# Softmax over rows of 512: sixteen equal chunks in two rings of buffers, replaced by seven unequal chunks worked in place in one array

## The chip, the cores and the metric

The kernel runs on one core of one Trainium2 chip. The metric is device microseconds for one execution of the kernel, taken as the median of several runs. A profile is a single execution; it has a span, from its first to its last instruction, and a time of its own, which is a little longer than the span.

## The reference

The input is 16 x 1024 rows of 512 float32 numbers, 33.55 MB. Each row is turned into its softmax, and an output of the same size is written.

```python
def reference(x: np.ndarray) -> np.ndarray:
    x_max = np.max(x, axis=-1, keepdims=True)
    exp_x = np.exp(x - x_max)
    return (exp_x / np.sum(exp_x, axis=-1, keepdims=True)).astype(np.float32)
```

## The kernel before, in words

The 16,384 rows are laid over 128 partitions, so each partition works on 128 rows. One "row" below means one row on every partition: 128 x 2 KB, 256 KB in HBM. The loop `for t in range(nchunks)` takes 16 chunks of R = 8 rows, 2 MB each. A chunk is contiguous in HBM, and a partition's share of it is one run of 16 KB.

For each chunk the loop records these steps, and the tile framework turns them into five instruction streams with semaphores between them:

- L47: SyncE (queue q1 of the profile) issues the load into `x_tile`, from a ring of 7 buffers.
- L49: GpSimd copies one column of the chunk into a guard tile. It waits for the load, and a later load of the same buffer waits for it.
- L61: ScalarE runs eight `activation` instructions, one for each row. Each computes exp of 512 numbers into `e_tile` (a ring of 4 buffers) and adds up the row in `accum_out`; the profile lists the reading of that sum as an instruction of its own. The bias is the constant 0.0: the maximum isn't subtracted, since `use_max` is off.
- L71, L74: VectorE takes the reciprocal of the eight sums, and multiplies all 4096 numbers of a partition by the broadcast reciprocals in one `tensor_mul`.
- L76: ScalarE's queue (q10) issues the store of `e_tile`.

After the loop, L80 has GpSimd write one column of the last four `e_tile` buffers, which waits for their stores. The framework's scheduler chooses the order on each engine: the built program has pairs of chunks on ScalarE, that is sixteen L61 instructions and then two stores. A load waits for the engines that read its buffer before, and a chunk's L61 waits until the store four chunks earlier has left its `e_tile`.

Of the kernel before, what the change touches and what calls it, by code (L numbers as in the profile page):

```python
# [2 lines left out]

# [4 lines left out]


@with_exitstack  # L10
def kernel(
    ctx: ExitStack,
    tc: tile.TileContext,
    x: bass.AP,
    out: bass.AP,
):
    nc = tc.nc
    P = nc.NUM_PARTITIONS

    x_flat = x.flatten_outer_dims()  # L20
    out_flat = out.flatten_outer_dims()
    n, d = x_flat.shape

    R = int(os.environ.get("SM_R", "8"))
    XBUFS = int(os.environ.get("SM_XBUFS", "7"))
    EBUFS = int(os.environ.get("SM_EBUFS", "4"))

    rows_per_chunk = P * R
    assert n % rows_per_chunk == 0
    nchunks = n // rows_per_chunk  # L30

    x_t = x_flat.rearrange("(t p r) d -> t p r d", p=P, r=R)
    out_t = out_flat.rearrange("(t p r) d -> t p r d", p=P, r=R)

    x_pool = ctx.enter_context(tc.tile_pool(name="xp", bufs=XBUFS))
    e_pool = ctx.enter_context(tc.tile_pool(name="ep", bufs=EBUFS))
    stats_pool = ctx.enter_context(tc.tile_pool(name="stats", bufs=12))
    guard_pool = ctx.enter_context(tc.tile_pool(name="guard", bufs=1))

    use_max = os.environ.get("SM_USEMAX", "0") == "1"  # L40

    guard_tile = guard_pool.tile([P, 1], mybir.dt.float32)

    e_tiles = []
    for t in range(nchunks):
        x_tile = x_pool.tile([P, R, d], mybir.dt.float32)
        nc.sync.dma_start(out=x_tile, in_=x_t[t])  # L47

        nc.gpsimd.tensor_copy(out=guard_tile, in_=x_tile[:, 0, 0:1])  # L49

        if use_max:
            neg_max = stats_pool.tile([P, R], mybir.dt.float32)
            nc.vector.reduce_max(
                out=neg_max, in_=x_tile, axis=mybir.AxisListType.X, negate=True
            )

        e_tile = e_pool.tile([P, R, d], mybir.dt.float32)
        e_tiles.append(e_tile)
        sums = stats_pool.tile([P, R], mybir.dt.float32)
        for r in range(R):  # L60
            nc.scalar.activation(  # L61
                out=e_tile[:, r, :],
                in_=x_tile[:, r, :],
                func=mybir.ActivationFunctionType.Exp,
                bias=neg_max[:, r : r + 1] if use_max else 0.0,
                scale=1.0,
                accum_out=sums[:, r : r + 1],
            )

        recip = stats_pool.tile([P, R], mybir.dt.float32)  # L70
        nc.vector.reciprocal(out=recip, in_=sums)  # L71

        recip_b = recip.unsqueeze(2).to_broadcast([P, R, d])
        nc.vector.tensor_mul(out=e_tile, in0=e_tile, in1=recip_b)  # L74

        nc.scalar.dma_start(out=out_t[t], in_=e_tile)  # L76

    for b in range(min(EBUFS, nchunks)):
        e_tile = e_tiles[nchunks - 1 - b]
        nc.gpsimd.memset(e_tile[:, 0, 0:1], 0.0)  # L80


# [1 line left out]
_INS = ['x']  # L84
_OUTS = [((16, 1024, 512), 'float32')]


# [23 lines left out]
```

## Time and profile before

| | before |
|---|---|
| median of 9 runs | 163.66 us (163.28 to 164.05) |
| the profiled execution's own time | 163.66 us |
| its span | 161.7 us |
| HBM read and written | 33.55 MB and 33.55 MB |
| VectorE busy | 74.0 us in 32 instructions |
| ScalarE busy | 80.7 us in 257 instructions |
| GpSimd busy | 13.7 us in 24 instructions |

How to read it: busy time is a sum over the span, and says little of what ends last. The page's second part cuts the span into 40 slices of 4.04 us; a digit is the busy share of a slice in tenths, "DMA" is the mean share of the core's 16 DMA engines, and "GB/s" is what these moved. The third part gives the share of each queue. The chain of the fourth part follows the last instruction back through what released it.

### The profile page before, as it was taken

Reading aid. Unit: us, or ns where it says so; the run is one execution under the profiler, and the core shown is the slowest. Engines: PE = TensorE matmul, PEld = TensorE weight load, DVE = VectorE, ACT = ScalarE, POOL = GpSimd, SP = SyncE. Lnnn points to the kernel's source line nnn. Section 1 sums busy time; section 2 is a strip of 40 time slices with the busy share of each in tenths; the row PEclk is TensorE's granted clock in tenths of the full one; section 3 lists DMA queues with packets and bytes.
Section 4 is the critical chain, followed back from the end, with each engine's and each line's share of the span. In section 5 each row is a group of like instructions: output and inputs, shape, how many; then the busy total and the mean of one; then the engine's idle time right before and its main releaser. Section 6 shows DMA issues by size and latency. Waiting matters only on the chain.

```text
span 161.7 us, 456 instructions
## 1 busy us (share of the span) xinstructions
DVE 74.0 (46%) x32; ACT 80.7 (50%) x257; POOL 13.7 (8%) x24
## 2 busy tenths in 40 slices
DVE  0006970994195509073000007950993399059700
ACT  3089519924883390910000099439915980896000
POOL 0000000024080000000000006300000000000000
DMA  5999999999999999999999999999999999999993
GB/s 154 430 434 418 442 341 440 434 426 434 430 422 442 430 426 438 422 434 442 422 434 442 422 430 442 422 434 432 430 434 426 430 438 426 430 434 426 434 438 154
DMA packets 4610, 67.13 MB, mean 415 GB/s; under 512 B 512, under 2 KB 512, under 8 KB 512
## 3 DMA queue, kind: packets, MB, share of 16 engines
q1 hardware_dynamic: 2304, 33.56, 49.4%
q10 hardware_dynamic: 2304, 33.56, 48.5%
q14 instruction: 2, 0.02, 0.0%
HBM read 33.55 MB, written 33.55 MB: 415 GB/s over the span
## 4 chain that ended last, share of the span: by engine, by line
DMA 52%; ACT 28%; DVE 17%; issue 1%; ACTq 1%; POOLq 0%; SPq 0%
DMA x_tile<-in_x_dram 35%; ACT e_tile L61 28%; DMA out_dram<-e_tile 17%; DVE e_tile L74 16%; DVE recip L71 1%; ACTq L76 1%; POOLq L106 0%; POOLq L80 0%; SPq L47 0%
## 5 line engine op out<-in xcount | busy, mean ns | idle before, releaser
L61 ACT ACTIVATE e_tile<-x_tile 128x512 f32<-128x512 f32 x128 | 78.5, 614 | 66.4 <-DMA x_tile<-in_x_dram 35.4
L74 DVE TENSOR_TENSOR e_tile<-e_tile,recip 128x4096 f32<-128x4096 f32 x16 | 70.8, 4425 | 0.6
L71 DVE RECIPROCAL recip<-sums 128x8 f32<-128x8 f32 x16 | 3.2, 203 | 78.0 <-ACT e_tile L61 78.0
L61 ACT ACTIVATION_READ_ACCUMULATOR e_tile<-x_tile 128x1 f32 x128 | 23.9, 187 | 0.0
L49 POOL COPY guard_tile<-x_tile 128x1 f32<-128x1 f32 x16 | 13.1, 819 | 124.1 <-DMA x_tile<-in_x_dram 124.1
L80 POOL MEMSET e_tile<- 128x1 f32 x4 | 0.4, 98 | 22.9 <-DMA out_dram<-e_tile 22.9
L61 ACT ACT_TABLE_LOAD x1 | 1.3, 1283 | 0.7 <-PEq L95 0.7
L95 POOL MEMSET const-float32-0.0<- 128x1 f32 x1 | 0.1, 98 | 0.2 <-issue 0.2
L95 POOL MEMSET const-bfloat16-1.0<- 128x1 bf16 x1 | 0.1, 101 | 0.0
L95 POOL MEMSET const-uint8-127<- 128x1 uint8 x1 | 0.1, 101 | 0.0
L95 POOL MEMSET const-float32-1.0<- 128x1 f32 x1 | 0.1, 98 | 0.0
## 6 DMA issues: line engine op xcount, KB each, us to landing
x_tile<-in_x_dram SPq DMA_DIRECT2D x16, 2048.0 KB, 42.3
out_dram<-e_tile ACTq DMA_DIRECT2D x16, 2048.0 KB, 17.9
```

The costliest lines, as they stand in the source:

```text
L49: nc.gpsimd.tensor_copy(out=guard_tile, in_=x_tile[:, 0, 0:1])
L61: nc.scalar.activation(out=e_tile[:, r, :], in_=x_tile[:, r, :], func=mybir.ActivationFunctionType.Exp, bias=neg_max[:, r : r + 1] if use_ ...
L71: nc.vector.reciprocal(out=recip, in_=sums)
L74: nc.vector.tensor_mul(out=e_tile, in0=e_tile, in1=recip_b)
L76: nc.scalar.dma_start(out=out_t[t], in_=e_tile)
L80: nc.gpsimd.memset(e_tile[:, 0, 0:1], 0.0)
L95: nc = _bacc.Bacc("TRN2", target_bir_lowering=False, num_devices=1)
```

## The change

The row maximum is computed and subtracted. The seven chunks have 3, 5, 9, 17, 31, 31 and 32 rows (`CHUNKS`: rows, and place in the array). One array `held` of 96 rows, 192 KB on each partition, holds the first six chunks side by side; the seventh lies over the first four (rows 0 to 31). A load is one DMA for a whole chunk, so a partition's run is 6 to 64 KB. Six loads are issued at the start (`EARLY`); the seventh is recorded behind the store of chunk 3 (`AFTER_STORE`).

Work is cut into groups of about eight rows: one each for chunks 0, 1 and 2, two for chunk 3 (8 and 9 rows), four for each of the last three (7, 8, 8, 8; the last 8, 8, 8, 8), 17 in all. `rowmax` is one VectorE reduction for a group, negated; `exps` is one `activation` for each row with that maximum as a bias read from memory, in place; `scale` is a reciprocal, and then one `tensor_scalar_mul` for each row, in place. The store of a chunk is issued from ScalarE's queue when its last group is scaled. The order is written out under `manual_schedule`: rowmax g, exps g, scale g-1. The GpSimd copies and memsets are gone.

In the built program VectorE has rowmax g, then the reciprocal and products of g-1, then rowmax g+1; ScalarE has the exponentials of g, then the store whose chunk ended with g-1. The seventh load waits on SyncE for the stores of chunks 0 to 3. The sixth waits there for the first load, whose semaphore it takes over. Waits go by the overlap of rows in `held`: rowmax waits for the load of its own chunk alone.

```diff
+CHUNKS = [(3, 0), (5, 3), (9, 8), (17, 17), (31, 34), (31, 65), (32, 0)]
+SBUF_ROWS = 96
+EARLY = 6
+AFTER_STORE = {3: [6]}
+GROUP = 8
...
+    held = data.tile([P, SBUF_ROWS, d], F32, name="held")
+    place = [held[:, s : s + R, :] for R, s in CHUNKS]
...
+        m = max(1, round(R / GROUP))
+        cuts = [R * i // m for i in range(m + 1)]
+        groups += [(k, a, b, b == R) for a, b in zip(cuts, cuts[1:])]
...
+    def load(k):
+        nc.sync.dma_start(out=place[k], in_=src[k])
...
+    def rowmax(g):
+        k, a, b, _ = groups[g]
+        shift[g] = stats.tile([P, b - a], F32, name="shift", tag="shift")
+        nc.vector.reduce_max(
+            out=shift[g], in_=place[k][:, a:b, :], axis=AX, negate=True
+        )
-        nc.gpsimd.tensor_copy(out=guard_tile, in_=x_tile[:, 0, 0:1])
...
+    def exps(g):
+        k, a, b, _ = groups[g]
+        sums[g] = stats.tile([P, b - a], F32, name="sums", tag="sums")
+        for r in range(a, b):
+            nc.scalar.activation(
+                out=place[k][:, r, :],
+                in_=place[k][:, r, :],
+                func=EXP,
+                bias=shift[g][:, r - a : r - a + 1],
+                scale=1.0,
+                accum_out=sums[g][:, r - a : r - a + 1],
             )
...
+    def scale(g):
+        k, a, b, last = groups[g]
+        recip = stats.tile([P, b - a], F32, name="recip", tag="recip")
+        nc.vector.reciprocal(out=recip, in_=sums[g])
+        for r in range(a, b):
+            nc.vector.tensor_scalar_mul(
+                out=place[k][:, r, :],
+                in0=place[k][:, r, :],
+                scalar1=recip[:, r - a : r - a + 1],
             )
+        if last:
+            nc.scalar.dma_start(out=dst[k], in_=place[k])
+            for later in AFTER_STORE.get(k, ()):
+                load(later)
 
-        recip_b = recip.unsqueeze(2).to_broadcast([P, R, d])
-        nc.vector.tensor_mul(out=e_tile, in0=e_tile, in1=recip_b)
-
-        nc.scalar.dma_start(out=out_t[t], in_=e_tile)
-
-    for b in range(min(EBUFS, nchunks)):
-        e_tile = e_tiles[nchunks - 1 - b]
-        nc.gpsimd.memset(e_tile[:, 0, 0:1], 0.0)
+    with tc.manual_schedule():
+        for k in range(EARLY):
+            load(k)
+        for g in range(len(groups)):
+            rowmax(g)
+            exps(g)
+            if g >= 1:
+                scale(g - 1)
+        scale(len(groups) - 1)
```

## The prediction

> **What bounds the kernel now.** I read the page's slices and queues first, then the chain, the waits of SyncE's queue, and the timeline for durations and landings.
>
> ```profile
> span 161.7 us, 456 instructions
> DVE 74.0 (46%) x32; ACT 80.7 (50%) x257; POOL 13.7 (8%) x24
> ...
> DMA  5999999999999999999999999999999999999993
> GB/s 154 430 434 418 442 341 440 434 426 434 430 422 442 430 426 438 422 434 442 422 434 442 422 430 442 422 434 432 430 434 426 430 438 426 430 434 426 434 438 154
> ...
> q1 hardware_dynamic: 2304, 33.56, 49.4%
> q10 hardware_dynamic: 2304, 33.56, 48.5%
> ...
> DMA 52%; ACT 28%; DVE 17%; issue 1%; ACTq 1%; POOLq 0%; SPq 0%
> ```
>
> The DMA engines are busy in every slice but the first and the last, and move about 431 GB/s whether they only load (the start), do both, or only store (the end). The kernel is bound by 67.1 MB through these engines. The chain gives ScalarE and VectorE 45%, but beside a DMA row that never falls these are only the route by which transfers hand on to each other. Hence two questions for any change: does it move fewer bytes (no), and does it ever leave the DMA engines without work?
>
> The timeline gives the pace:
>
> ```profile
> 13.50 0.18 POOL L49 COPY guard_tile<-x_tile 128x1 f32<-128x1 f32 x1 [4.76 <-DMA x_tile<-in_x_dram]
> ...
> 18.39 0.18 POOL L49 COPY guard_tile<-x_tile 128x1 f32<-128x1 f32 x1 [4.71 <-DMA x_tile<-in_x_dram]
> ...
> 18.71 4.42 DVE L74 TENSOR_TENSOR e_tile<-e_tile,recip 128x4096 f32<-128x4096 f32 x1
> ...
> 155.94 0.10 POOL L80 MEMSET e_tile<- 128x1 f32 x1 [4.75 <-DMA out_dram<-e_tile]
> 160.78 0.10 POOL L80 MEMSET e_tile<- 128x1 f32 x1 [4.75 <-DMA out_dram<-e_tile]
> ```
>
> Loads land 4.89 us apart, stores 4.84: eight rows, so 0.608 us for a row of 256 KB in either direction. The second load (16 rows) is seen at 13.50, so n rows are seen at 3.8 + 0.608 n. All 256 give 159.4; the last store is seen at 160.7. About 0.8 us of the difference is the slice of 341 GB/s, where the first store starts ((430 - 341)/430 of 4.04 us). The span ends 1.0 us after that store. So the most that a better order could gain here is about 1 us.
>
> **What the skill says.** "DMA: Bandwidth & Descriptors", section on queues, rings and completion order: a DMA engine takes turns between its queues packet by packet. The packet records agree: each packet is 16 KB, lasts 0.61 us, and loads and stores alternate one for one. The same page, "Where 436 GB/s comes from", puts the ceiling at 435 GB/s; 431 agrees. "VectorE: DVE Perf Modes", tier table: a float32 product with a scalar runs at two elements a cycle, a reduction at one; this trace shows neither operation.
>
> **The change part by part.**
>
> GpSimd's copies and memsets go: its share of the chain is 0%, so 0 to 0.1 us.
>
> Exponentials: L61 starts every 0.61 us. "ScalarE: Activation LUTs", on what ACT_TABLE_LOAD costs, has 186 + 0.833 x 512 = 613 ns for constant operands (the trace: 614) and 93 ns more for a bias read from memory. No row shows that; bounds 0.61 and 0.70, I take 0.70, so 5.7 us for eight rows with the last sum.
>
> Row maximum: no row. The nearest is L74, the same 4096 elements at one a cycle: 4.43 us for eight rows, 3.9 for seven; a little less is possible, not below 4.27.
>
> Scaling: a product of 512 is 267 ns at two elements a cycle, plus 75 ns an instruction by section 5.2 of "Vector Engine (DVE) Microarchitecture Reference": an estimate of 0.34 us. Without the doubled rate it is 0.61; slightly faster, 0.33. With the reciprocal (0.24 in the trace): 3.0 us for eight rows, 2.6 for seven, 3.3 for nine.
>
> So VectorE needs 7.4 us and ScalarE 5.7 for eight rows, whose two transfers take 9.7. On average all hides. What doesn't is the order: I walk it.
>
> *Until the seventh load.* Loads of 6 to 62 KB a partition run back to back. Stores 0 and 1 are short packets (6 and 10 KB) that alternate with 34 and 62 KB ones, so they hardly slow the loads. Chunk 4 is complete after 65 loaded rows and about 7 stored: 3.8 + 0.8 + 0.608 x 72 = 48.4. Its first rowmax stands on VectorE ahead of the scaling of chunk 3's second group: the added wait, behind which the store of chunk 3 is queued. 48.4 + 3.9 = 52.3; scaling to 55.6; but ScalarE has seven exponentials ahead of the store, which is issued at about 57. Chunk 5 (31 rows) and stores 2 and 3 keep the DMA engines full meanwhile. Store 3 is the last of 96 + 34 = 130 rows, seen at 3.8 + 0.8 + 0.608 x 130 = 83.6.
>
> *First hole.* Only then is the seventh load issued. Before, the first load's first packet came 1.0 us after its issue (0.73, 1.73), and a landing is seen 0.4 to 1 us after its last byte: 1.6 us idle, up to 3.0 if the slow first packets of a start recur (1.4). I take 2: the load runs from 85.0. Is another store ready by then? VectorE from 55.6: rowmax, scaling in turn, 4.43 + 2.6 + 4.43 + 3.0 + 4.43 + 3.0 = 77.5; rowmax of chunk 5 to 81.4; scaling of chunk 4's last group to 84.4; ScalarE's exponentials end at 86.4, then store 4 is issued. It isn't ready.
>
> *When the seventh load lands.* Its 32 rows alone would take 19.5 us; with store 4 it alternates packet for packet, at half speed. In the packet records a store issued at 92.4 beside a busy load queue starts at 95.9, about 2.5 us later than an idle one would: four packets of 16 KB. If that lag is one of bytes or time, store 4 starts at 90.0, when the load has moved 8.2 rows; the other 23.8 take 29: landed 118.9, seen 119.4. If four packets pass ahead whatever their size (four of 64 KB, 9.4 us), it starts at 97, and the load is seen at 112.4. I take 115.5 between them.
>
> *From there to the end* nothing is left to load, and everything hangs on 32 rows of arithmetic: on VectorE four rowmax (17.7), three scalings (9.0), then the last exponentials (5.7) and the last scaling (3.0): 35.4 us. Then issue to first packet 1.0, the last store of 32 rows 19.5, uneven ends and landing 1.1, tail 1.0: seen landing + 58.0. What hides it is stores 4 and 5, 62 rows or 37.7 us, but half of store 4 has run beside the load, and store 5 is issued only behind chunk 6's first exponentials, landing + 10.2 = 125.7, while store 4 is through at 85 + 63 x 0.608 = 123.3 (*second hole*, 3.4 us with the first packet). Store 5 ends at 126.7 + 18.9 = 145.6; store 6 starts at 115.5 + 35.4 + 1 = 151.9: *third hole*, 6.3 us.
>
> The sum: 115.5 + 58.0 = 173.5 us of span. Checked by holes: 161.7 + 2 + 3.4 + 6.3 = 173.4. The profiled time stands 2.0 us over its span and equals the median of the runs: 163.66 + 11.8 = 175.5 us. With the ends of the lag, 172.4 and 179.4; the smaller costs (first hole 1.6 to 3.0, exponential 0.61 to 0.70, product 0.33 to 0.40) move that by about 2 either way.
>
> **Rivals.**
>
> 1. *The load is served first.* If all eight packets that an engine has of the seventh load pass ahead of store 4, it lands at 104.5. VectorE, with 5b to 5d still to do, reaches chunk 6 at about 106.4, and stores 4 and 5 cover the arithmetic: 106.4 + 58 = 164.4, or 166.4 us. For it: a lag exists. Against: it was four packets, not eight.
>
> 2. *The products run at one element a cycle.* Each scaling grows by 0.27 us a row. VectorE becomes the bound: 63 rows before chunk 6 put its start at 106.4 + 17 = 123.4, and the last 32 rows add 8.6: 123.4 + 58.0 + 8.6 = 190, or 192 us. For it: no such instruction in the trace; against: the tier table.
>
> 3. *The other side: longer runs move faster.* If runs of 62 KB went through at over 431 GB/s, every transfer would shrink. The moved rows on the path to the end are some 130 + 57 + 32 = 219, 133 us; 11.8 us off that needs 9%, so from about 473 GB/s the kernel would not be slower; there the time is 163.5. For it: fewer packets. Against: 431 is constant in all stages, at the page's ceiling.
>
> **Chances.** Holes as forecast 0.74 (alone 170.5 to 181.5); load first 0.12; slow products 0.07; faster transfers 0.04; another cause that closes the holes 0.03. A change of 0.2% is about what can be told from none. Faster 0.03, the same 0.03, slower 0.94. The range 168.0 to 181.5 takes in the lag's two ends and part of rival 1; it leaves out the rest of that, and rivals 2 and 3.
>
> **What would show it.** The DMA row should have three holes, near 83, 123 and 146 us, the last the widest; slices between them should stay near 431 GB/s. The chain should end with a store of some 20 us behind about 35 us of VectorE and ScalarE. Products at 0.34 us apart and exponentials at 0.70 bear the prices out. A seventh load that lands before 107 us, or a DMA row without holes, proves me wrong.

## The result, and the profile after

| | before | changed |
|---|---|---|
| median | 163.58 us (31 runs, 163.28 to 164.05) | 184.41 us (10 runs, 184.18 to 185.64) |
| ratio to before | | 1.128 (95% interval 1.1267 to 1.1293) |
| span of the profiled execution | 161.7 us | 182.9 us |
| moved, mean over the span | 415 GB/s | 367 GB/s |

The kernel became slower, as forecast, but by 20.8 us where 11.8 were forecast, and outside the range (168.0 to 181.5).

The page of the changed kernel: span, slices, queues and the chain by engine. A slice is now 4.57 us, and slices are numbered from 0. A packet of 62 or 64 KB lasts 2.4 us and is counted in the slice in which it starts, so single slices jump up and down; zeros and runs of low slices count.

```profile
span 182.9 us, 502 instructions
...
DVE  0579539992299999999999990008999999520000
ACT  0752953949037669597496874000859577400000
...
DMA  6999999998979899987799999981099990096995
GB/s 231 421 444 395 425 465 409 514 470 306 506 321 491 367 489 393 423 373 245 229 452 452 453 452 452 437 389 69 0 444 444 444 444 0 0 416 272 459 459 229
...
q1 hardware_dynamic: 1008, 33.55, 44.3%
q10 hardware_dynamic: 1008, 33.55, 42.5%
...
DMA 62%; DVE 17%; ACT 5%; issue 2%; SPq 1%; DVEq 0%; ACTq 0%
```

The DMA row has three holes where it had none: a shallow one in slices 18 and 19 (82 to 91 us), then slices 27 and 28 (123 to 133), then 33 and 34 (151 to 160). VectorE's and ScalarE's rows tell the cause. Both have three zeros just ahead of the second hole (slices 24 to 26, and 25 to 27): they wait for one load, while store 4 runs out. In the second hole VectorE is at 8 and 9, in the third at 9 and 5, and nothing is ready to be stored. The last slices are the other way round: only the last store runs.

The chain in order of time says the same. Columns: start, duration, what.

```profile
49.07 3.90 DVE shift L65
...
56.80 27.90 DMA out_dram<-held
84.70 0.02 SPq L60
84.72 0.04 issue
84.76 39.42 DMA held<-in_x_dram
124.18 0.02 issue
124.20 4.42 DVE shift L65
...
147.48 4.34 DVE shift L65
...
151.91 5.76 ACT held L73 x16
```

Store 3 ends at 84.7, the seventh load is issued at 84.76 and lands 39.4 us later, and from 124.2 the chain is the arithmetic of the last 32 rows. The timeline shows where it ends, and the groups what the new operations cost:

```profile
161.22 0.34 ACTq L93 DMA_DIRECT2D out_dram<-held  x1
```

```profile
L73 ACT ACTIVATE held<-held,shift 128x512 f32<-128x512 f32 x128 | 90.6, 708 | 59.0 <-DVE shift L65 55.6
L65 DVE TENSOR_REDUCE shift<-held 128x8 f32<-128x4096 f32 (+4 forms) x17 | 70.8, 4164 | 34.1 <-DMA held<-in_x_dram 34.1
L87 DVE TENSOR_SCALAR held<-held,recip 128x512 f32<-128x512 f32 x128 | 52.2, 482 | 0.6
```

The last store is issued at 161.2, 37.0 us after the landing, and is the only transfer to the end. VectorE's work grew by 50 us (124.0 against 74.0), but its idle time before maxima, 34.1 us, is all put down to loads: the engine isn't the bound over the span, it is late in one place.

### The profile page after: what moved, and what is told of

It reads as the page before. It is cut to its first block, busy times and chain, and to the rows that moved or that the text cites. A ratio compares the mean times of both kernels' runs of the same rounds, so it can differ in the third digit from the quotient of the medians.

```text
span 182.9 us, 502 instructions
## 1 busy us (share of the span) xinstructions
DVE 124.0 (68%) x162; ACT 93.4 (51%) x257; POOL 0.2 (0%) x4
## 4 chain that ended last, share of the span: by engine, by line
DMA 62%; DVE 17%; ACT 5%; issue 2%; SPq 1%; DVEq 0%; ACTq 0%
DMA held<-in_x_dram 47%; DMA out_dram<-held 15%; DVE shift L65 10%; DVE held L87 7%; ACT held L73 5%; SPq L60 1%; DVE recip L85 0%; DVEq L131 0%; ACTq L73 0%
## 5 line engine op out<-in xcount | busy, mean ns | idle before, releaser
L73 ACT ACTIVATE held<-held,shift 128x512 f32<-128x512 f32 x128 | 90.6, 708 | 59.0 <-DVE shift L65 55.6
L65 DVE TENSOR_REDUCE shift<-held 128x8 f32<-128x4096 f32 (+4 forms) x17 | 70.8, 4164 | 34.1 <-DMA held<-in_x_dram 34.1
L87 DVE TENSOR_SCALAR held<-held,recip 128x512 f32<-128x512 f32 x128 | 52.2, 482 | 0.6
L73 ACT ACTIVATION_READ_ACCUMULATOR held<-held,shift 128x1 f32 x128 | 23.8, 186 | 0.0
L85 DVE RECIPROCAL recip<-sums 128x8 f32<-128x8 f32 (+4 forms) x17 | 3.3, 192 | 2.5 <-ACT held L73 2.5
```

Of the source, the lines that this page charges most:

```text
L65: nc.vector.reduce_max(out=shift[g], in_=place[k][:, a:b, :], axis=AX, negate=True)
L73: nc.scalar.activation(out=place[k][:, r, :], in_=place[k][:, r, :], func=EXP, bias=shift[g][:, r - a : r - a + 1], scale=1.0, accum_out=s ...
L85: nc.vector.reciprocal(out=recip, in_=sums[g])
L87: nc.vector.tensor_scalar_mul(out=place[k][:, r, :], in0=place[k][:, r, :], scalar1=recip[:, r - a : r - a + 1],)
```

## The experiments

Three theories are put against each other. *Order*: the DMA engines stand idle around the last chunk, because its load waits for stores, lands as one piece and late, and is stored as one piece. *Arithmetic*: the added work on VectorE costs the time wherever it stands. *Large transfers*: runs of 62 KB move badly in themselves. Ratios are to the kernel before on the same chip, with their 95% intervals.

### The last store in four pieces (e1)

```diff
+        if k == 6:
+            nc.scalar.dma_start(out=dst[k][:, a:b, :], in_=place[k][:, a:b, :])
-        if last:
+        elif last:
```

> The last chunk is stored in four pieces of eight rows, each when its group is scaled. Theory of the order (the loss is idle DMA around the last chunk): its landing stays at 124 us; its pieces follow store 5 from 152 us with no gap (152 to 162, 166.5, 171.3), so the span is about 172.6 us and the time about 174.2 us, 10 us less. Theory of the arithmetic (47 us of maxima and slower products on VectorE are what costs): nothing is removed from VectorE, the time stays within 2 us of 184.4. Theory of the large transfers (runs of 62 KB move badly): only the last chunk's store changes to 16 KB runs, 1 to 3 us less.

Measured: 174.14 us, ratio 1.066 (1.0629 to 1.0691), span 172.3. The load is seen at 123.8, the pieces are stored from 151.3 to 171.1 us without a gap. The third hole was worth 10.3 us; arithmetic and its order on VectorE are the same to the instruction. The first and second hole stay.

### Equal chunks, same arithmetic (e2)

```diff
-CHUNKS = [(3, 0), (5, 3), (9, 8), (17, 17), (31, 34), (31, 65), (32, 0)]
+CHUNKS = [(8, 8 * (k % 12)) for k in range(16)]
-EARLY = 6
-AFTER_STORE = {3: [6]}
+EARLY = 12
+AFTER_STORE = {k: [k + 12] for k in range(4)}
```

> Same arithmetic, same array and order, but sixteen chunks of eight rows in a ring of twelve places. Theory of the order: no load waits long for a store, no hole in the DMA row, 163 to 164.5 us. Theory of the arithmetic: it is all still there, so 175 us or more. Theory of the large transfers: back to 163 to 165 us too, since runs are 16 KB again.

Measured: 163.07 us, ratio 0.9973 (0.9963 to 0.9983). Its page:

```profile
span 161.2 us, 527 instructions
DVE 123.8 (77%) x160; ACT 93.2 (58%) x257; POOL 0.2 (0%) x4
...
DMA  5999999999999999999999999999999999999994
```

VectorE has the same 124 us of work as in the changed kernel, and the DMA row is as full as before the change. The theory of the arithmetic is gone, as far as the amount of work goes. Order and large transfers both survive this one.

### A store held back (e3)

```diff
-        if last:
+        if last and k != 4:
...
             exps(g)
+            if groups[g][0] == 5 and groups[g][3]:
+                nc.scalar.dma_start(out=dst[4], in_=place[4])
             if g >= 1:
                 scale(g - 1)
```

> The store of chunk 4 is issued behind the exponentials of chunk 5's last group and not as soon as chunk 4 is scaled, so the seventh load has the engines to itself. Theory of the order: the load is seen at about 107.5 us and not at 124; store 4 goes out at 112, VectorE comes to the last chunk at 109.6, the last store runs from 151 to 170.4: span about 171.7 us, time about 173.2 us, though a store was only delayed. Theory of the arithmetic: no change, 184 us. Theory of the large transfers: no change or slower, since the same transfers start later.

Measured: 169.96 us, ratio 1.0388 (1.0372 to 1.0403), span 168.2. Store 4 was issued at 107.8, when the third of the eight exponentials ahead of it in the program had just started, and not behind the last, as I had assumed; so the hole before it was shorter than expected. No transfer was made smaller and one is issued 21 us later, yet 14.4 us are gone, and the last load alone moves 434 GB/s (90 to 102 us): the theory of the large transfers falls. The issues of the seventh load in both kernels, first of the changed one, then of this one (last number: us to landing):

```profile
held<-in_x_dram SPq DMA_DIRECT2D x1, 39.4
```

```profile
held<-in_x_dram SPq DMA_DIRECT2D x1, 22.0
```

From issue to landing 22.0 us alone, 39.4 beside store 4. The packet records add a detail: alone, the last byte arrives at 106.24 and the landing comes at 106.67; beside store 4 the last byte arrives at 121.38 and the landing at 124.18. The load's count of completion comes 2.8 us behind its data, not 0.43. The records show why: behind its data each engine has a packet of 4 bytes on the load's queue, and 0.4 us after each of these the load's semaphore rises by one. Alone, this packet starts as the engine's last data packet ends; beside store 4 it starts 2.33 us later, in the median of the 16 engines, and a store packet of 62 KB lasts 2.34. The count takes its turn behind one store packet. So it does in the runs e1, e5, e6 and e11, where a store still runs as the last load ends (2.33 to 2.41 us); in e7, where store 4 is over by then, nothing comes between.

### The maximum alone, in the kernel before (e4)

```diff
-    use_max = os.environ.get("SM_USEMAX", "0") == "1"
+    use_max = os.environ.get("SM_USEMAX", "1") == "1"
```

> The kernel before with its own switch for the row maximum on: one reduction of 4096 for each chunk (4.4 us, 71 us in all) on VectorE, and a bias read from memory in each exponential. Theory of the order: VectorE has 145 us of work beside 156 us of transfers, which hide it unless it comes late for a store: 163.5 to 166 us. Theory of the arithmetic: 175 us or more.

Measured: 179.91 us, ratio 1.1002 (1.0986 to 1.1018). My expectation missed by 14 us. The profile of this run, slices first and then VectorE's timeline:

```profile
DVE  0189899999994689999999999997992279667910
...
DMA  6999999999999999999999999998259619687974
```

```profile
76.07 4.42 DVE L74 TENSOR_TENSOR e_tile<-e_tile,recip 128x4096 f32<-128x4096 f32 x1
80.41 17.39 DVE L53 TENSOR_REDUCE neg_max<-x_tile 128x8 f32<-128x4096 f32 x4
97.72 0.19 DVE L71 RECIPROCAL recip<-sums 128x8 f32<-128x8 f32 x1
```

The scheduler puts four maxima in a row ahead of the next product, so 17.4 us pass on VectorE in which no chunk becomes ready to be stored. ScalarE waits for products 48.5 us in all (total, times, longest):

```profile
ACT e_tile L61 <- DVE e_tile L74: 48.5, 5, 19.0
```

So exponentials are left over at the end: from 135.3 us on, those of the last five chunks run one chunk in 6.0 us where a store takes 4.84, and the stores run dry; the first low slices are 27 to 29. In the equal chunks above, with maxima and products in turn, 124 us of VectorE's work cost nothing; here it has 142, and the buffers differ too. That the order is what costs is thus read from the trace, and no run changed it alone. The theory of the arithmetic was right in part for the old order.

### A last chunk of 31 rows (e5)

```diff
-CHUNKS = [(3, 0), (5, 3), (9, 8), (17, 17), (31, 34), (31, 65), (32, 0)]
-SBUF_ROWS = 96
+CHUNKS = [(3, 0), (5, 3), (9, 8), (17, 17), (32, 34), (31, 66), (31, 0)]
+SBUF_ROWS = 97
```

> One row moves from the last chunk to chunk 4 (32, 31, 31). In the changed kernel the first two packets that each engine loads of the last chunk move 19 to 21 GB/s and not 27. Theory of the restart (a load queue that stood idle for 14 us starts slowly): the same here, first two packets near 20 GB/s. Theory of the pitch (partitions that lie exactly 64 KB apart in HBM are slow): full speed from the first packet, the landing 1.7 us earlier still. In either case the last chunk has one row less of arithmetic (about 1.0 us) and of transfers (0.6 to 1.2 us) on the path to the end: about 182.3 us with a slow restart, 180.6 without.

Measured: 183.76 us, ratio 1.1236 (1.1215 to 1.1258). The first packet of each engine moved 20.7 GB/s in the mean, the second 27.0, the third 18.1 on 14 of the 16 engines, the later ones 27.1. So partitions exactly 64 KB apart are not the cause; nor are the first two packets the slow ones, as the theory of the restart had it. The slow third one is the last ahead of store 4, whose first packets come at 94.7 to 95.9 us on these engines. On the two others they came at 91.8 and 92.0, ahead of the load's third packet; these two ended their part of the load at 121.7, 2 us behind the rest, and the load was seen at 124.5 only. That is why the time is above both expectations.

### The wait ahead of store 3 taken away (e6)

```diff
+            first = groups[g][0] == 4 and groups[g][1] == 0
+            if first:
+                scale(g - 1)
             rowmax(g)
             exps(g)
-            if g >= 1:
+            if g >= 1 and not first:
                 scale(g - 1)
```

> At chunk 4's first group VectorE scales chunk 3's last group before it waits for chunk 4, so the wait that the prediction called the added one is gone, and store 3 is issued some 8 us earlier (about 48 us). Theory of the order as the packet records of the changed kernel show it: store 3 stood behind store 2 on its queue until 71.8 us anyway, so nothing later moves: 184.4 us within 0.5. Theory of the prediction (that wait is part of the loss): up to 8 us less.

Measured: 186.63 us in one run, 195.35 to 195.75 in the three others; the profile is of one of these three. No gain, but not "nothing later moves" either. Store 3 is issued at 49.6 and not at 56.8, and its packets still start at 71.6 us (71.7 in the changed kernel), behind store 2: so far as expected. But store 4 is now issued at 84.30 us, in the same moment as the seventh load (84.31), and gets its first packets at 88.7 and not at 92.1. From then to 129 us both move 369 GB/s together where the changed kernel has 434 (93 to 118 us):

```profile
GB/s 245 424 474 393 406 481 454 457 354 413 458 348 466 508 336 454 360 231 399 359 332 362 387 400 293 374 278 13 0 210 420 420 420 210 0 217 433 433 433 217
```

Slices 18 to 25 (of 4.84 us) are those of the two transfers. The load is seen at 134.9, 10.7 us later than in the changed kernel, and the span is 10.7 us longer. The end of this run hangs on that landing. Why the pair moves so slowly stays open, and the run of 186.63 us left no profile.

### No maximum (e7)

```diff
-                bias=shift[g][:, r - a : r - a + 1],
+                bias=0.0,
...
-            rowmax(g)
             exps(g)
```

> The maximum is left out (no reduction, bias 0.0), so this kernel computes the softmax without subtracting the maximum. Theory of the order: VectorE has half the work, store 4 is issued at about 72 us and follows store 3 without a gap (no first hole), but then it shares the engines with the seventh load, which is seen at 122 to 125 us again; from there ScalarE's 32 exponentials (19.6) and the last scaling (3.5) take 23 us where it was 37: span about 168 to 170 us, time 170 to 172, still 7 us over the kernel before. Theory of the arithmetic: with that work gone, 164 us.

Measured: 168.76 us, ratio 1.0318 (1.0303 to 1.0334), span 167.2. With VectorE's work cut from 124.0 to 55.7 us, 5 us above the kernel before remain.

```profile
span 167.2 us, 478 instructions
DVE 55.7 (33%) x145; ACT 80.4 (48%) x257; POOL 0.2 (0%) x4
...
ACT  3574804990007999806999800000079999000000
...
DMA  5999899797998979999999799989559599099955
```

ScalarE's six zeros in slices 23 to 28 are the wait for the seventh load, on which again all the rest hangs. That load was seen at 122.1 us as expected, and the last store was issued 23.3 us later (145.48). The maximum and its bias cost 15.6 us in this chunking: of the 15.7 by which the spans differ, 13.7 lie between landing and last issue (37.0 against 23.3), which the stores don't cover, and 2.0 in the earlier landing. Where stores cover them, as in the equal chunks, they cost nothing. This run also shows that the load need not start slowly: it began while store 4 was running, and its packets moved 27.1 GB/s from the first.

### The seventh load in four pieces (e8)

```diff
-        nc.sync.dma_start(out=place[k], in_=src[k])
+        if k == 6:
+            for a in range(0, 32, 8):
+                nc.sync.dma_start(
+                    out=place[k][:, a : a + 8, :], in_=src[k][:, a : a + 8, :]
+                )
+        else:
+            nc.sync.dma_start(out=place[k], in_=src[k])
```

> The seventh load is issued as four loads of eight rows, each waiting for the stores that its own rows lie over. Theory of the order: the first piece is there before VectorE is through with chunk 5 (109.5 us), the first and second holes close, VectorE runs on without a pause and the last store is issued at about 146.5: span about 168.2 us, time about 170 us, with one hole of some 8 us left before the last store. Theory of the large transfers: the other transfers are unchanged, 182 us or more.

Measured: 172.8 and 173.0 us in two runs, 178.8 in two; the profile is of a run at 178.8 (span 177.0). The first piece is issued at 54.5 us and VectorE runs on into the last chunk at 109.4, so the first two holes are gone, as expected. But the fourth piece ends only at 138.9 us in this profile, and VectorE stands 8.9 us before it:

```profile
141.58 4.42 DVE L71 TENSOR_REDUCE shift<-held 128x8 f32<-128x4096 f32 x1 [8.88 <-DMA held<-in_x_dram]
```

From 123 us on three of the 16 DMA engines, at last one, still have rows of the last piece, in packets of 16 KB that start 2.95 us apart: each has a 62 KB packet of store 5 ahead of it. Small packets beside large ones lose their share, and the slowest engine decides. In direction the theory held, in size it missed by 3 to 9 us; the runs at 173 left no profile.

### Load and store of the last chunk in pieces (e9)

Both edits (the load in four pieces, the last store in four pieces) together.

> The last chunk is loaded and stored in four pieces of eight rows; nothing else of the changed kernel is touched. Theory of the order: no hole wider than 2 us is left, because stores of pieces fill the one before the last store: span 161.5 to 163.5 us, time 163.5 to 165.5 us, so the whole loss lies in handling the last 32 rows as one unit. Theory of the arithmetic: 175 us or more.

Measured: 165.64 us, ratio 1.0122 (1.0096 to 1.0147), a little above the expectation. Of the 20.8 us, 18.8 are gone with the first six chunks left as they are; what the other 2.0 are was not tried.

### Sizes: eight chunks of 16 (e10), four of 32 (e11), small ends (e12)

```diff
-CHUNKS = [(3, 0), (5, 3), (9, 8), (17, 17), (31, 34), (31, 65), (32, 0)]
+CHUNKS = [(16, 16 * (k % 6)) for k in range(8)]
...
-AFTER_STORE = {3: [6]}
+AFTER_STORE = {0: [6], 1: [7]}
```

> Eight chunks of sixteen rows in a ring of six places, runs of 32 KB. Theory of the order: the loads that wait for a store (the seventh and eighth) find other loads queued ahead, and 16 rows of arithmetic (22 us with the last exponentials) are covered by waiting stores: no hole, and runs of over 30 KB move 433 GB/s where 16 KB moved 431: 162.2 to 163.0 us. Theory of the large transfers: slower than the 163.07 us of chunks of eight.

Measured: 162.28 us, ratio 0.9921 (0.9909 to 0.9933): the fastest of all, with the maximum subtracted.

```profile
span 160.6 us, 498 instructions
...
DMA  7999999999999999999999999999999999999993
```

```diff
-CHUNKS = [(3, 0), (5, 3), (9, 8), (17, 17), (31, 34), (31, 65), (32, 0)]
+CHUNKS = [(32, 32 * (k % 3)) for k in range(4)]
...
-EARLY = 6
-AFTER_STORE = {3: [6]}
+EARLY = 3
+AFTER_STORE = {0: [3]}
```

> Four chunks of 32 rows in a ring of three places. Theory of the order: first store at about 61 us, when the three first loads are done; the fourth load waits for it until 81 us, then shares the engines with the second store; the third store is gone before the fourth chunk is scaled: 178 to 183 us. Theory of the large transfers (only their rate counts): 433 GB/s as with 31 rows, within 2 us of chunks of sixteen.

Measured: 175.36 us, ratio 1.0717 (1.0702 to 1.0733). The hole before the last store is back (slices 33 and 34), and so is the one before the load that waits (slice 18); the fourth load, issued at 82.1, was more than half through when store 1 joined at 96.9, and landed at 115.5; the two shared the engines for a part of it only, and the time is below the expectation.

```profile
DMA  7999599995999969990999988999699950099595
```

```diff
-CHUNKS = [(3, 0), (5, 3), (9, 8), (17, 17), (31, 34), (31, 65), (32, 0)]
+CHUNKS = [(4, 0), (4, 4), (8, 8), (16, 16), (16, 32), (16, 48), (16, 64), (16, 80)]
+CHUNKS += [(16, 0), (8, 16), (4, 24), (4, 28)]
...
-EARLY = 6
-AFTER_STORE = {3: [6]}
+EARLY = 8
+AFTER_STORE = {2: [8], 3: [9, 10, 11]}
```

> Chunks of 4, 4, 8, six of 16, 8, 4 and 4 rows. Theory of the order: as with chunks of sixteen there is no hole; small chunks at the ends can shorten only the uneven end of the last transfers and nothing in the middle: 162.0 to 163.0 us. If small chunks beside large ones lose their turn to the large packets, a late load of the last pieces could open a hole: 163.5 us or more.

Measured: 162.79 us, ratio 0.995 (0.9935 to 0.9965). No hole, and nothing won over plain chunks of 16.

## Why the prediction was wrong

**What held.** The bound (a DMA row that must never fall), the sign, the cause, the three holes near their places, and the rejection of the rivals: no faster transfers, no load served first. The first landing of the walk was within 0.7 us: chunk 4 seen at 49.07 (48.4 worked out). Store 3 was over at 84.7 (83.6), store 4 was issued at 86.80 (86.4).

**The step that failed** is "When the seventh load lands", 115.5 us in the sum and 124.2 in the profile: 8.7 of the 9.4 us by which the span was missed (182.9 against 173.5). Two lines of the timeline, store 4's issue and a group of eight products, go with what follows:

```profile
86.80 0.34 ACTq L93 DMA_DIRECT2D out_dram<-held  x1
...
128.77 3.26 DVE L87 TENSOR_SCALAR held<-held,recip 128x512 f32<-128x512 f32 x8
```

The step has three parts.

- *The choice between the lag's two ends: 3.9 us.* "If four packets pass ahead whatever their size" was one end, a lag of bytes or time the other, and I took the middle. In the changed kernel store 4's first packet came 5.3 us after its issue (86.80 to 92.09), when each engine had moved two packets of the load: eight rows, as the end of bytes or time had it (8.2 rows, load seen at 119.4). That the rows agree so well is luck: that end had store 4 start at 90.0 beside a load at full rate, and it started later, beside a slower one. The lag is neither four packets nor a fixed time: 3.5 us in the kernel before, 5.3 here, 6.3 in e11. The e3 run, with store 4 held back, shows how much hangs on it: 17.5 us of landing, 14.4 us of time.
- *A late and slow start of the load: 2.5 us.* I had the load run from 85.0. Its first packet came at 85.73, though only 1.4 us after the last byte of store 3, since store 3 was over 1.1 us late. And the first two packets of each engine moved 20.9 and 19.3 GB/s: 6.5 us where 27.1 GB/s give 4.8. So the last byte arrived at 121.4 and not at 118.9. I had the slow first packets of the kernel's own start as an upper end, 1.4 us, and took 0.4 of it. Only the first packet belongs to the start: in e3, where no store follows, the second moves 27.1. The second is the last ahead of store 4's first packet, as the slow third one in e5 and a slow fifth one in e11 (17.6).
- *The count behind the data: 2.3 us.* I had 0.5 us from last byte to landing; it was 2.8, with a packet of store 4 ahead of the count on each engine.

**The arithmetic behind it** was mis-sized by 1.6 us: 37.0 from landing to the last issue, where 35.4 was worked out. The products are the term: eight take 3.26 us, 0.41 each where I had 0.34. Over four groups that is 2.2 us; 0.6 came back, since a maximum starts before the products ahead of it have ended. The Trainium skill's price in "Vector Engine (DVE) Microarchitecture Reference", section 5.2 (75 ns an instruction, measured there at one element a cycle) is too low here: 0.41 less the streaming of 0.267 leaves 0.14. The skill's "VectorE: DVE Perf Modes", tier table, is borne out in that products run at two elements a cycle: a maximum, at one a cycle, takes 4.41 us for 4096 elements, which is 0.55 for 512. Maximum (4.41 against 4.43) and exponential (0.708 long, eight with the last sum 5.76 against 5.7) were right, the latter as the skill's "ScalarE: Activation LUTs", on what ACT_TABLE_LOAD costs, has it. The tail, from issue of the last store to the end, was 21.7 against 22.6: -0.9. Sum: 8.7 + 1.6 - 0.9 = 9.4.

**By holes:** 1.4 us and 1.7 of slow packets (2 worked out), 6.8 from 126.06 to 132.90 (3.4), 10.2 from 151.85 to 162.06 (6.3): 20.1, against 11.7. The remaining 1.1 us of the span's 21.2 is there when store 3 ends (84.7, where the pace of the kernel before gave 83.6).

**What was right for a wrong reason:** "the added wait, behind which the store of chunk 3 is queued". The wait is there, but store 3 stood behind store 2 on its own queue until 71.7 us: stores 1 and 2, eight packets on each engine, took turns with eight of 62 KB, so that store 1, of 5 rows, ran from 32.0 to 51.8. With the wait gone, e6 left store 3 where it was. That such stores "hardly slow the loads" was right; that the loads slow them wasn't drawn out.

**The range** took in both ends of the lag, but slow start, count and products all fell on the far side of the far end, where I had left 2 us.

## What to carry to other kernels

In a kernel bound by transfers, look not at how much work an engine gets but at the last chunk: from its landing on, its arithmetic must be covered by stores that are already waiting, so its size times the arithmetic of a row has to be less than that backlog, and it should be loaded, scaled and stored in pieces. A load whose place is freed by a store should find other loads queued ahead of it, as with chunks of 16 in six places; where it starts beside a large store, the two take turns packet by packet, and holding the store back can be the faster order (e3). A gain of longer runs is there, but small: a ratio of 0.9973 to the kernel before with runs of 16 KB, 0.9921 with 32 KB, and the rates below differ by as much.

## What the runs showed of the hardware

- Packets are as long as a partition's run, here 6 to 64 KB. With the engines full, in loads, stores and both, 16 KB packets moved 431 GB/s in all, 32 KB ones 433, 62 and 64 KB ones 433 to 434.
- Queues take turns by packet and not by bytes: store 0 of 3 rows (6 KB packets), beside loads of 34 and then 62 KB, took 11.9 us (16.53 to 28.45) for 0.8 MB.
- The count that reports a load is a packet of 4 bytes on each engine, and takes its turn like any other: it started 2.33 to 2.41 us after the engine's last data beside a store of 62 or 64 KB packets (the changed kernel, e1, e5, e6, e11), at once without one (e3, e7).
- A load that started while all engines were idle had a slow first packet on each engine in every such run here (20.9 GB/s in the changed kernel, 21.6 in e1, 21.8 in e3, 20.7 in e5, 19.1 in e6, 21.3 in e11; the start of each kernel too), and moved at the full 27.1 when it started beside a store (e7). Stores after a hole lose little (26.7 in the changed kernel). The mechanism wasn't tried.
- A load that ran alone had another slow packet just ahead of the first packet of a store in four runs (19.3 in the changed kernel, 19.0 in e1, 18.1 in e5, 17.6 in e11), and so at the first store of the kernel before (17.5 at 20.6 to 22.8 us), but not ahead of its store at 95.9 us (26.8). This too stays open.
